# Stationary weights for the grouped queries and the indexer, 512-column scores, and weight conversions ranked 1,000 instructions ahead, in a four-layer hybrid decoder on one core

## The chip, the core and the metric

The kernel runs on one core of a Trainium2 chip. The metric is device time in microseconds (us). TensorE (PE in the rows, PEld for its weight loads) does the matrix products, VectorE (DVE) and ScalarE (ACT) the elementwise work, GpSimd (POOL) and SyncE (SP) issue most of the DMAs.

## The reference

Four layers run on a sequence of 256 tokens of width 2048, with mixers in the order latent attention, sparse attention, sliding window, latent attention. All is float32.

```python
for i in range(DEPTH):                      # 4 layers
    h = rmsnorm(x, norm_in[i])
    # kind 0: latent attention; kind 1: sparse (indexer + top-k); kind 2: window of 128
    self_out, mq, gate = mixer(h @ w_in)    # 32 heads of 64 (kinds 1, 2) or 16 of 128 (kind 0)
    mem_out = memory_attention(mq, mem_n @ w_mem_kv[i])   # 4 heads of 256
    y = concatenate([self_out, mem_out]) * silu(gate)
    x = x + y @ w_out[i]
out = rmsnorm(x, final_norm)

# indexer of kind 1: 16 heads of 64, one shared key
dots  = einsum('bqhd,bkd->bqhk', iq, ik) * 64 ** -0.5
score = einsum('bqhk,bqh->bqk', relu(dots), iw) * 16 ** -0.5
# a query sees its best 64 keys under the causal mask
```

## The kernel before

**Split products.** Each float32 operand is split in a high part of type float32r (11 mantissa bits) and the rest, and a product of two operands is three float32r products: high by high, high by low, low by high. For weights, `parts_of` (L234) does it: ACT copies a 128x512 piece of the landed tile `wr` to `wh` (L60, called by `split`), and DVE writes `wl = wr - wh` (L69). `wh` and `wl` have three buffers each; a piece is converted into a buffer when the products that read the piece three before it are done.

**Two ways to project.** `rows_by` (L240) holds the activations stationary and moves 512 columns of weights: six products of 512 columns for each 128 rows of weights. Its result has tokens on the partitions, and what attention needs with features on the partitions goes through transposes. `columns_by` (L270) holds 128 columns of weights stationary and moves the 256 tokens: for `wh` the high and low part of the tokens in one product of 512 columns (L285), for `wl` the high part alone, 256 columns (L289). Its result has features on the partitions.

**Order.** A layer is six parts: memory heads (part 4), four groups of self heads (0 to 3), memory heads (part 5). A part is a projection with its gate (`project`, `gate`), an attention (`attend`), and one part later its share of the output projection (`w_out`, L1141), which reads the part's gated output `y`: four steps of 128 rows of `w_out`, of which the first two need the first half of `y`, the last two the second half. The program is not run in the order written: a scheduler orders each engine's instructions by a priority that follows the written order and by what is ready in its own model. So the attention of one part lies between the projection and output products of its neighbours. Each engine then runs its list strictly in that order.

**Attention.** `masked_softmax` (L515) works on two blocks of 128 queries, `b` = 0 and 1: score on PE, add of the bias and minimum on DVE (L529), exponential on ACT, reciprocal on DVE, scaling on ACT, then three transposes on PE (L502, tile `ptp`), a split of the transposed weights (tiles `pT`, `pT2`), and the products with the values (tile `o`). For block 0 the score moves both key parts in one product of 256 columns and DVE adds the two halves (L527); for block 1 it is two products of 256 columns into the same columns. `memory_attend` (L576) does six products of 256 columns for each block.

**Grouped layers** (`Grouped`, kinds 1 and 2). `project` (L925) uses `rows_by` for the 512 query columns of a group (tile `acc_q`), ACT scales the rows, and `four_heads` (L461) transposes them in float32 and splits. The indexer (`select`, L817) projects its 1024 query columns with `rows_by` in three calls of 512, 256 and 336 columns (tile `acc_iq`; the last carries the keys and the head weights); for the first two calls the first 64 tokens, which need no selection, are left out. `stacked`, `stacked_late` and `dup` split and transpose.

Of the kernel before, what the change touches and what calls it, by code (L numbers as in the profile page):

```python
# [31 lines left out]
def kernel(ctx: ExitStack, tc: tile.TileContext, a: dict, out: bass.AP,  # L32
# [20 lines left out]
    def f32(ap):  # L53
        return ap.bitcast(F32)
# [185 lines left out]
    def rows_by(xt, kts, w, k0, cols, name, prepare=None, each=None, late=None):  # L240
# [3 lines left out]
        for s in range(0, kts, ST):  # L244
# [3 lines left out]
            for k in range(m):  # L248
# [4 lines left out]
                for t in range(2):  # L253
                    xh, xl = (q[:, v, (s + k) % 4, t * P:(t + 1) * P] for v in range(2))
                    first, last = s + k == 0, s + k == kts - 1
                    if late is not None and t == 0:

                        both = late[:, s + k].rearrange("p v c -> p (v c)")
                        if not last:
                            nc.tensor.matmul(acc[t][:, :n], both, wh[:, :n], start=first, stop=False)  # L260
                        nc.tensor.matmul(acc[t][:64, :n], both[:, :64], wl[:, :n], start=False, stop=False)
                        if last:
                            nc.tensor.matmul(acc[t][:, :n], both, wh[:, :n], start=False, stop=True)
                        continue
# [43 lines left out]
    class Norm:  # L308
# [37 lines left out]
        def finish(self):  # L346
# [5 lines left out]
            nc.vector.tensor_scalar(self.eighth, self.rstd, 0.125, None, op0=OP.mult)  # L352
            half = small("xh", 2)
# [161 lines left out]
    def masked_softmax(score, bias, scale=None, nsk=None):  # L515
# [5 lines left out]
        for b in range(2):  # L521
# [54 lines left out]
    def memory_attend(nm, kT, v, qT, gT):  # L576
        y = act.tile([P, 2, 4, S], F32R, name="y", tag="y", bufs=2)
        for h in range(2):
            es = []
            mn, sm = small("mn", 2), small("sm", 2)  # L580
            for b in range(2):
                sp = misc("msp")
                qs = slice(b * P, (b + 1) * P)
                seq = [(qT[h][:, u, k, qs], kT[h][:, v_, k, :])
                       for k in range(2) for u, v_ in ((0, 0), (0, 1), (1, 0))]
                for n_, (l, r_) in enumerate(seq):
                    nc.tensor.matmul(sp[:, :S], l, r_, start=n_ == 0, stop=n_ == len(seq) - 1)
                nc.vector.tensor_reduce(mn[:, b:b + 1], sp[:, :S], AX.X, OP.max, negate=True)
# [3 lines left out]
                nc.scalar.activation(e, sp[:, :S], AF.Exp, bias=ms[:, :1], scale=nm.col("rstd", b),  # L592
# [640 lines left out]
```

## Time and profile before

| | |
|---|---|
| device time, median of 3 runs | 2577.18 us (2577.11 to 2577.99) |
| span of the profiled execution | 2575.1 us |
| PE busy | 2564.1 us |
| PEld busy | 2208.4 us |
| DVE busy | 1906.1 us |
| ACT busy | 1621.0 us |
| DMA | 520.02 MB, mean 202 GB/s |

The span runs from the first to the last instruction of one profiled execution; no other time of that execution is given, and the median of the runs is 2.1 us more than the span, for what lies around it. PE is busy in all but 11 us of it. A busy PE is one with products in flight; how fast they follow each other is read from their starts.

### The profile page before, as it was taken

The numbers are of one execution on the slowest core, as the hardware profiler recorded it, in microseconds if no ns is written. First come the engines' busy times: TensorE is split into PE (matmuls) and PEld (weight loads), VectorE is DVE, ScalarE is ACT, GpSimd is POOL, SyncE is SP. The second block draws the span as 40 slices with busy tenths as digits, with TensorE's granted clock in tenths as the row PEclk, the third lists the DMA queues.
The fourth block names the chain that finished last, engine by engine and source line by source line (L and its number), as shares of the span: only waits on it lengthen the run. The fifth ranks groups of instructions, "written<-read, shape, count | busy, mean of one in ns | idle before, by whom it ended". The sixth has DMA issues, their size and how long they took to land. (4 is left out here: it accounts for less than half of the span.)

```text
span 2575.1 us, 41628 instructions
## 1 busy us (share of the span) xinstructions
PE 2564.1 (100%) x13986; PEld 2208.4 (86%) x13986; DVE 1906.1 (74%) x4179; ACT 1621.0 (63%) x3467; POOL 87.1 (3%) x159
## 2 busy tenths in 40 slices
PE   9999999999999999999999999999999999999998
PEld 7888898888888888888888888888889888888887
DVE  6666667677777786887778776787878767777776
ACT  6556556556656566667666666676766655665665
POOL 1000000000000000000000000000000000000000
PEclk9999999999999999999999999999999999999999
DMA  9888777666676667566656575555655877676664
GB/s 303 258 259 267 239 212 235 185 170 191 196 201 201 203 213 246 173 197 188 196 165 197 170 226 170 169 183 185 196 156 148 241 201 198 196 196 181 212 173 179
DMA packets 459416, 520.02 MB, mean 202 GB/s; under 512 B 69520, under 2 KB 353056, under 8 KB 457536
## 3 DMA queue, kind: packets, MB, share of 16 engines
q1 hardware_dynamic: 441744, 449.72, 58.3%
q0 software_dynamic: 16736, 66.65, 8.0%
q8 instruction: 110, 1.80, 0.3%
q14 instruction: 106, 0.87, 0.1%
q10 hardware_dynamic: 720, 0.98, 0.1%
HBM read 494.10 MB, written 35.75 MB: 206 GB/s over the span
## 5 line engine op out<-in xcount | busy, mean ns | idle before, releaser
L69 DVE TENSOR_TENSOR wl<-wr,wh 128x512 fp32r<-128x512 f32 (+2 forms) x1720 | 1159.4, 677 | 579.1 <-ACT wh L60 555.5
L60 ACT ACTIVATE wh<-wr 128x512 fp32r<-128x512 f32 (+2 forms) x1720 | 1064.9, 621 | 801.7 <-PE acc_g L285 166.9
L285 PE MATMUL acc_g<-xT,wh 128*128 128x512 f32 x1536 | 484.7, 396 | 0.0
L289 PEld LDWEIGHTS acc_g<-xT,wl 128*128 128x128 f32 x1536 | 284.6, 188 | 63.0
L289 PE MATMUL acc_g<-xT,wl 128*128 128x256 f32 x1536 | 304.6, 280 | 0.0
L266 PE MATMUL acc_wo<-wl,y 128*128 128x512 f32 x752 | 297.3, 395 | 0.3 <-DVE wl L69 0.3
L267 PE MATMUL acc_wo<-wh,y 128*128 128x512 f32 x752 | 292.4, 390 | 0.0
L285 PEld LDWEIGHTS acc_g<-xT,wh 128*128 128x128 f32 x1536 | 235.9, 189 | 1.3
L265 PE MATMUL acc_wo<-wh,y 128*128 128x512 f32 x752 | 234.9, 392 | 0.1
L266 PEld LDWEIGHTS acc_wo<-wl,y 128*128 128x128 f32 x752 | 141.3, 188 | 28.5 <-DVE wl L69 1.2
L267 PEld LDWEIGHTS acc_wo<-wh,y 128*128 128x128 f32 x752 | 141.4, 188 | 27.1
L265 PEld LDWEIGHTS acc_wo<-wh,y 128*128 128x128 f32 x752 | 139.3, 188 | 28.5 <-ACT y L60 1.0
L285 PE MATMUL acc_mk<-mT,wh 128*128 128x512 f32 x512 | 161.5, 396 | 0.4 <-ACT wh L60 0.4
L285 PE MATMUL acc_mq<-xT,wh 128*128 128x512 f32 x512 | 161.6, 396 | 0.0
L1146 DVE TENSOR_TENSOR x<-x,acc_wo 128x512 f32<-128x512 f32 x184 | 122.3, 682 | 4.0 <-PE acc_wo L267 3.6
L285 PE MATMUL acc_qn<-cT,wh 128*128 128x512 f32 x384 | 121.3, 397 | 0.0
L285 PE MATMUL acc_cq<-xT,wh 128*128 128x512 f32 x384 | 120.9, 396 | 0.0
L289 PEld LDWEIGHTS acc_mk<-mT,wl 128*128 128x128 f32 x512 | 96.1, 188 | 22.8 <-DVE wl L69 0.4
L289 PEld LDWEIGHTS acc_mq<-xT,wl 128*128 128x128 f32 x512 | 93.7, 188 | 19.6
L289 PE MATMUL acc_mq<-xT,wl 128*128 128x256 f32 x512 | 103.4, 282 | 0.0
L266 PE MATMUL acc_q<-wl,xT 128*128 128x512 f32 x256 | 101.4, 396 | 0.0
L289 PE MATMUL acc_mk<-mT,wl 128*128 128x256 f32 x512 | 101.1, 278 | 0.0
(335 smaller groups left out, 4349.5 us busy)
## 6 DMA issues: line engine op xcount, KB each, us to landing
wr<-in_w_out_dram SPq DMA_DIRECT2D x188, 512.0 KB, 3.7
wr<-in_w_in_a_dram SPq DMA_DIRECT2D x176, 512.0 KB, 4.0
wr<-in_w_mem_kv_dram SPq DMA_DIRECT2D x120, 512.0 KB, 4.5
wr<-in_w_in_b_dram SPq DMA_DIRECT2D x112, 512.0 KB, 3.5
wr<-in_w_in_c_dram SPq DMA_DIRECT2D x104, 512.0 KB, 3.5
wr<-in_w_uq_dram SPq DMA_DIRECT2D x192, 128.0 KB, 2.9
wr<-in_w_uq_dram SPq DMA_DIRECT2D x48, 256.0 KB, 3.8
tab<-flat POOLq DMA_DIRECT2D x8, 1536.0 KB, 9.1
```

The costliest lines, as they stand in the source:

```text
L60: inst = nc.scalar.activation(o, i, AF.Copy, scale=scale)
L69: nc.vector.tensor_sub(lo, src, f32(hi))
L265: nc.tensor.matmul(acc[t][:, :n], xh, wh[:, :n], start=first, stop=False)
L266: nc.tensor.matmul(acc[t][:, :n], xh, wl[:, :n], start=False, stop=False)
L267: nc.tensor.matmul(acc[t][:, :n], xl, wh[:, :n], start=False, stop=last)
L285: nc.tensor.matmul(acc[j], wh[:, o:o + P], q[:, :, kt % 4, :], start=kt == 0, stop=False)
L289: nc.tensor.matmul(acc[j][:, 0, :], wl[:, o:o + P], q[:, 0, kt % 4, :], start=False, stop=kt == kts - 1)
L1146: nc.vector.tensor_add(xs, xs, acc[t])
```

## The change

`Grouped.project` calls `columns_by` twice for the 512 query columns and a new `heads_by_columns`, which adds the two halves of the result, scales and splits them; the float32 transposes of the queries go. The indexer calls a new `columns_of`, which is `columns_by` with a list of column tiles and a first token for each: 384 and 192 moving columns for the query tiles (tokens 64 to 255), 512 and 256 for the tile with keys and head weights. Scores of block 1 move both key parts in one product of 512 columns, and DVE adds the halves (in `memory_attend` after a copy on ACT). The instructions of `parts_of` get a rank 1,000 instructions earlier than their place in the program.

```diff
 def parts_of(wr, c0, n):
     ...
-        split(wh[:, :n], wl[:, :n], wr[:, c0:c0 + n])
+        with tc.high_priority(offset=1000):
+            split(wh[:, :n], wl[:, :n], wr[:, c0:c0 + n])
...
+    def columns_of(xt, kts, w, c0, tiles, name):
+
+        acc = [ps.tile([P, 512], F32, name=f"acc_{name}{j}", tag="acc", bufs=4) for j in range(len(tiles))]
+        n = tiles[-1][0] + tiles[-1][1]
+        per, each = ST * 512 // n, 512 // n
+        for s in range(0, kts, per):
+            m = min(per, kts - s)
+            wr, _ = stage(w, s, m, (c0, n))
+            other_work()
+            for k2 in range(0, m, each):
+                wh, wl = parts_of(wr, k2 * n, each * n)
+                for k in range(each):
+                    kt = s + k2 + k
+                    q = xt[kt // 4]
+                    for (o, width, r0), at in zip(tiles, acc):
+                        nc.tensor.matmul(at[:width, :2 * (S - r0)], wh[:, k * n + o:k * n + o + width],
+                                         q[:, :, kt % 4, r0:], start=kt == 0, stop=False)
+                    for (o, width, r0), at in zip(tiles, acc):
+                        nc.tensor.matmul(at[:width, :S - r0], wl[:, k * n + o:k * n + o + width],
+                                         q[:, 0, kt % 4, r0:], start=False, stop=kt == kts - 1)
+        return acc
...
 masked_softmax
-            if b == 0:
-                nc.vector.tensor_add(u[:, :n], sp[:, n:2 * n], bi)
-                bi = u[:, :n]
-            nc.vector.tensor_tensor_reduce(u[:, :n], sp[:, :n], bi, -1.0,
+            nc.vector.tensor_add(u[:, :n], sp[:, n:2 * n], bi)
+            nc.vector.tensor_tensor_reduce(u[:, :n], sp[:, :n], u[:, :n], -1.0,
...
 memory_attend
-                seq = [(qT[h][:, u, k, qs], kT[h][:, v_, k, :])
-                       for k in range(2) for u, v_ in ((0, 0), (0, 1), (1, 0))]
...
+                for k in range(2):
+                    nc.tensor.matmul(sp, qT[h][:, 0, k, qs], kT[h][:, :, k, :], start=k == 0, stop=False)
+                    nc.tensor.matmul(sp[:, :S], qT[h][:, 1, k, qs], kT[h][:, 0, k, :], start=False, stop=k == 1)
+                u = wk.tile([P, S], F32, name="u", tag="e", bufs=4)
+                copy_act(u, sp[:, S:])
+                nc.vector.tensor_tensor_reduce(u, sp[:, :S], u, -1.0, BIG,
...
 Latent.attend, block 1
-                        seq = [(q[:, 0, z, qs], k[:, 0, z, :]), (q[:, 0, z, qs], k[:, 1, z, :]),
-                               (q[:, 1, z, qs], k[:, 0, z, :]),
-                               (qr[:, h, qs], self.kr[:, 0, :]), (qr[:, h, qs], self.kr[:, 1, :])]
+                        seq = [(q[:, 0, z, qs], k[:, :, z, :]), (q[:, 1, z, qs], k[:, 0, z, :]),
+                               (qr[:, h, qs], self.kr)]
...
 Grouped.select (stacked, stacked_late and late_x go)
+            for h0 in range(0, 16, 4):
+                tiles = [(0, P, 64), (P, P, 64)] + ([(S, 80, 0)] if h0 == 12 else [])
+                acc = columns_of(nm.at, 16, w, 2560 + h0 * 64, tiles, "iq")
...
+        def heads_by_columns(self, dst, acc):
+
+            zs = part_tile(F32)[:].rearrange("p (j c) -> p j c", j=2)
+            for j in range(2):
+                copy_act(zs[:, j, :], acc[j][:, 1, :])
+                nc.vector.tensor_add(zs[:, j, :], zs[:, j, :], acc[j][:, 0, :])
+            eighth = self.nm.half[:, None, :].to_broadcast([P, 2, S])
+            nc.vector.scalar_tensor_tensor(zs, zs, 0.25, eighth, op0=OP.mult, op1=OP.mult)
+            for h, main, low in ((0, slice(0, 64), slice(64, P)), (1, slice(64, P), slice(0, 64))):
+                copy_act(dst[main, h::2, :], zs[main])
+                nc.vector.tensor_sub(dst[low, h::2, :], zs[main], f32(dst)[main, h::2, :])
+
         def project(self, g):
             nm = self.nm
-            acc = rows_by(nm.at, 16, self.w, 0, (g * 512, 512), "q")
...
             for z in range(2):
-                rows_ = part_tile(F32)
-                for t in range(2):
-                    copy_act(rows_[:, t * S:(t + 1) * S], acc[t][:, z * S:(z + 1) * S],
-                             scale=nm.col("eighth", t))
-                four_heads(q[z], [rows_[:, t * S:(t + 1) * S] for t in range(2)])
+                acc = columns_by(nm.at, 16, self.w, 0, (g * 512 + z * S, S), "q")
+                self.heads_by_columns(q[z], acc)
...
 Grouped.attend
-                    if b == 0:
-                        nc.tensor.matmul(sp[:, :S], qb, self.k[:, g, :, :P], start=True, stop=True)
-                    else:
-                        for v in range(2):
-                            nc.tensor.matmul(sp[:, :S], qb, self.k[:, g, v, :],
-                                             start=v == 0, stop=v == 1)
+                    n = (b + 1) * P
+                    nc.tensor.matmul(sp[:, :2 * n], qb, self.k[:, g, :, :n], start=True, stop=True)
```

The built programs show how the scheduler's order moves. The first place is PE in the sparse layer, where one part's output projection begins (`acc_wo`; `y_13987` before and `y_13980` after are that part's output, `o_14191` and `o_14184` the values' products of its last heads). Before:

```order
L979 MATMUL o_14191<-pT2_14227,vz_12691 128x512
L979 MATMUL o_14191<-pT2_14226,vz_12692 128x512
L979 MATMUL o_14191<-pT2_14226,vz_12691 128x256
L979 MATMUL o_14191<-pT2_14227,vz_12691 128x256
L979 MATMUL o_14191<-pT2_14226,vz_12692 128x256
L950 MATMUL sp_14919<-kd_11111,qS_14643 128x256
L285 MATMUL acc_g0_14794<-xT_10871,wh_14888 128x512
L285 MATMUL acc_g1_14795<-xT_10871,wh_14888 128x512
L953 MATMUL sp_14928<-kd_11111,qS_14643 128x256 x2
L265 MATMUL acc_wo0_15199<-wh_15203,y_13987 128x512
```

After the change, at the same transition, in the second step of the output projection and behind it:

```order
L259 MATMUL acc_wo1_15223<-wh_15236,y_13980 128x512
L257 MATMUL acc_wo0_15270<-wh_15274,y_13980 128x512
L258 MATMUL acc_wo0_15270<-wl_15275,y_13980 128x512
L259 MATMUL acc_wo0_15270<-wh_15274,y_13980 128x512
L518 MATMUL ptp_14247<-ident_81,e_14232 128x128
L951 MATMUL sp_14942<-kd_11099,qS_14458 128x256
L951 MATMUL sp_14951<-kd_11099,qS_14458 128x512
L518 MATMUL ptp_14247<-ident_81,e_14241 128x128 x2
L257 MATMUL acc_wo1_15271<-wh_15274,y_13980 128x512
L258 MATMUL acc_wo1_15271<-wl_15275,y_13980 128x512
L259 MATMUL acc_wo1_15271<-wh_15274,y_13980 128x512
L976 MATMUL o_14184<-pT2_14219,vz_12654 128x512
```

Before, the last heads' value products stand ahead of the part's first output product; after, two steps of the output projection and the start of another column (`acc_wo0_15270`) stand ahead of them, and steps three and four of the first column follow later.

The second place is ACT at the same transition. Before:

```order
L60 ACTIVATE wh_14888<-wr_14874 128x512
L60 ACTIVATE wh_15203<-wr_15201 128x512
L60 ACTIVATE wh_15213<-wr_15201 128x512
L60 ACTIVATE y_13987<-yt_14266 128x512
L60 ACTIVATE wh_15225<-wr_15223 128x512
L60 ACTIVATE z_14900<-acc_g0_14794 128x256
L60 ACTIVATE wh_15235<-wr_15223 128x512
```

After:

```order
L60 ACTIVATE wh_15236<-wr_15224 128x512
L60 ACTIVATE wh_15248<-wr_15246 128x512
L60 ACTIVATE z_14923<-acc_g0_14817 128x256
L60 ACTIVATE pT2_14219<-ptp_14215 128x3x128
L60 ACTIVATE wh_15258<-wr_15246 128x512
L548 ACTIVATE e_14232,sm_14224<-u_14227,mn_14223 128x128
L60 ACTIVATE wh_15274<-wr_15272 128x512
L548 ACTIVATE e_14241,sm_14224<-u_14236,mn_14223 128x256
```

Here `wh_15248` and `wh_15258` are steps three and four of the first column. They are converted ahead of the exponentials of the last heads (`e_14232`, `e_14241`), from which the second half of `y` comes, and `wh_15274` then takes the buffer of `wh_15236`.

## Rows read from the trace of the kernel before

**Rows 1.** The page: engine totals, granted clock in 40 slices.
```profile
PE 2564.1 (100%) x13986; PEld 2208.4 (86%) x13986; DVE 1906.1 (74%) x4179; ACT 1621.0 (63%) x3467; POOL 87.1 (3%) x159
...
PEclk9999999999999999999999999999999999999999
```

**Rows 2.** All waits of PE: what waited for what, us in total, times, longest.
```profile
PE wu L102 <- DVE ones L98: 1.1, 1, 1.1
PE acc_mv L265 <- ACT wh L60: 0.6, 1, 0.6
PE acc_mk L285 <- ACT wh L60: 0.4, 1, 0.4
PE acc_wo L266 <- DVE wl L69: 0.3, 2, 0.2
```

**Rows 3.** Two windows, 96 row products (acc_mv) and 128 column products (acc_mk).
```profile
98.46:120.25 21.79, 21.79 (x98) 18.03 (x97) 13.69 (x24) 12.65 (x24) 0.53 (x1) 1.00 0.78 264
120.25:142.53 22.28, 22.28 (x129) 19.45 (x128) 15.12 (x27) 13.73 (x28) 1.59 (x3) 1.00 0.85 262
```

**Rows 4.** Timeline of PE: float32 transposes between products (start us, us, what).
```profile
1226.75 0.49 PE L502 MATMUL ptp<-ident,e 128*128 128x128 f32 x3
...
1227.32 0.39 PE L267 MATMUL acc_wo<-wh,y 128*128 128x512 f32 x1
```

**Rows 5.** Counts: query products and float32 transposes of the grouped layers.
```profile
L266 PE MATMUL acc_q<-wl,xT 128*128 128x512 f32 x256 | 101.4, 396 | 0.0
...
L467 PE MATMUL tr<-ident,hl 128*128 128x128 f32 x64 | 8.9, 272 | 0.0
```

**Rows 6.** Timeline of PE in the indexer, 336 columns; then of PEld, two loads.
```profile
1018.05 0.32 PE L267 MATMUL acc_iq<-wh,xT 128*128 128x336 f32 x1
...
1019.89 0.32 PE L267 MATMUL acc_iq<-wh,xT 128*128 128x336 f32 x1
...
1017.48 0.19 PEld L266 LDWEIGHTS acc_iq<-wl,xT 128*128 128x128 f32 x1
1017.59 0.19 PEld L267 LDWEIGHTS acc_iq<-wh,xT 128*128 128x128 f32 x1
```

**Rows 7.** Timeline of PE, ACT and DVE where the sparse layer ends.
```profile
1440.24 0.39 PE L267 MATMUL acc_wo<-wh,y 128*128 128x512 f32 x1
1440.46 1.23 PE L979 MATMUL o<-pT,vz 128*128 128x512 f32 x6
1441.53 0.64 PE L265 MATMUL acc_wo<-wh,y 128*128 128x512 f32 x2
1442.32 0.51 PE L266 MATMUL acc_wo<-wl,y 128*128 128x512 f32 x1 [0.15 <-DVE wl L69]
1442.66 0.39 PE L267 MATMUL acc_wo<-wh,y 128*128 128x512 f32 x1
...
1443.12 0.40 PE L267 MATMUL acc_wo<-wh,y 128*128 128x512 f32 x1
1443.58 0.50 PE L265 MATMUL acc_wo<-wh,y 128*128 128x512 f32 x1
...
1440.71 0.64 ACT L60 ACTIVATE wh<-wr 128x512 fp32r<-128x512 f32 x1 [0.20 <-ACT th L483]
...
1441.58 0.68 DVE L69 TENSOR_TENSOR wl<-wr,wh 128x512 fp32r<-128x512 f32 x1
```

**Rows 8.** Timeline of PE and ACT: one head from score to scaled weights, little queued.
```profile
1187.16 0.40 PE L953 MATMUL sp<-kd,qS 128*128 128x256 f32 x2
1187.40 0.40 PE L289 MATMUL acc_g<-xT,wl 128*128 128x256 f32 x2
...
1190.19 0.80 ACT L60 ACTIVATE e<-e,rc 128x128 f32<-128x128 f32 x2 [0.23 <-DVE rc L552]
```

**Rows 9.** Groups of DVE: the add of a bias and a score, 256 columns.
```profile
L962 DVE TENSOR_TENSOR bs<-bm,vs 128x256 f32<-128x256 f32 x32 | 13.4, 417 | 0.0
```

**Rows 10.** Window over two parts of the sparse layer.
```profile
1136.00:1300.00 164.00, 164.00 (x850) 139.07 (x850) 131.45 (x319) 112.80 (x259) 3.94 (x6) 1.00 0.63 198
```

More of the change, by code (lines that the diff above doesn't have):

```diff
@@ L255, in rows_by @@
                     first, last = s + k == 0, s + k == kts - 1
[L256 to L264, printed above, removed]
                     nc.tensor.matmul(acc[t][:, :n], xh, wh[:, :n], start=first, stop=False)
@@ L352, in finish @@
             nc.vector.tensor_scalar(self.eighth, self.rstd, 0.125, None, op0=OP.mult)
+            self.neg = small("xn", 2, bufs=3)
+            nc.vector.tensor_scalar(self.neg, self.rstd, -1.0, None, op0=OP.mult)
             half = small("xh", 2)
@@ L583, in memory_attend @@
                 qs = slice(b * P, (b + 1) * P)
-                seq = [(qT[h][:, u, k, qs], kT[h][:, v_, k, :])
-                       for k in range(2) for u, v_ in ((0, 0), (0, 1), (1, 0))]
-                for n_, (l, r_) in enumerate(seq):
-                    nc.tensor.matmul(sp[:, :S], l, r_, start=n_ == 0, stop=n_ == len(seq) - 1)
-                nc.vector.tensor_reduce(mn[:, b:b + 1], sp[:, :S], AX.X, OP.max, negate=True)
+                for k in range(2):
[4 more added lines that the diff above has]
+                nc.vector.tensor_tensor_reduce(u, sp[:, :S], u, -1.0, BIG,
+                                               op0=OP.add, op1=OP.min, accum_out=mn[:, b:b + 1])
                 ms = small("ms", 2)
@@ L737, in score @@
                     else:
[L738 to L740 removed]
+                        seq = [(q[:, 0, z, qs], k[:, :, z, :]), (q[:, 1, z, qs], k[:, 0, z, :]),
+                               (qr[:, h, qs], self.kr)]
                     for n_, (l, r_) in enumerate(seq):
[L742 removed]
+                        n = r_.shape[-1] * (r_.shape[1] if len(r_.shape) == 3 else 1)
+                        nc.tensor.matmul(sp[:, :n], l, r_, start=n_ == 0, stop=n_ == 2)
                     return sp
@@ L852, in select, with indexer_keys @@
             return self.selection(iqT, ikd, iw, iw2)
-        def stacked_late(self, dst, src, sc, n):
-            s64 = small("s64", 1)
-            nc.scalar.activation(s64[:64], sc[64:], AF.Copy)
-            lo = tmp("lo")
-            nc.scalar.activation(lo[:64, :n * 64], src[64:], AF.Copy)
-            z = tmp("zq")
-            nc.vector.tensor_add(z[:64, :n * 64], lo[:64, :n * 64], src[:64])
-            s3 = z[:64, :n * 64].rearrange("p (g d) -> p g d", g=n)
-            for g0 in range(0, n, 4):
-                hl = part_tile()[:64].rearrange("p (g v d) -> p g v d", g=4, v=2)
-                copy_act(hl[:, :, 0, :], s3[:, g0:g0 + 4], scale=s64[:64])
-                nc.vector.scalar_tensor_tensor(hl[:, :, 1, :], s3[:, g0:g0 + 4], s64[:64], f32(hl)[:, :, 0, :],
-                                               op0=OP.mult, op1=OP.subtract)
-                tp = misc("tr", F32R)
-                for g in range(4):
-                    nc.tensor.transpose(tp[:, g * 64:g * 64 + 64], hl[:, g].rearrange("p a b -> p (a b)"),
-                                        identr[:64, :64])
-                copy_act(dst(g0, g0 + 4), f32(tp)[:, :S].rearrange("p (j c) -> p j c", c=64))
+        def indexer_keys(self, ikd, iw, acc):
+            nm = self.nm
+            z = wk.tile([P, S], F32, name="z", tag="z", bufs=3)
+            copy_act(z[:80], acc[:80, S:])
+            nc.vector.tensor_add(z[:80], z[:80], acc[:80, :S])
+            tp = misc("tp")
+            for t in range(2):
+                nc.tensor.transpose(tp[:, t * P:t * P + 80], z[:80, t * P:(t + 1) * P], ident[:80, :80])
+            for t in range(2):
+                copy_act(iw[:, t * 16:(t + 1) * 16], tp[:, t * P + 64:t * P + 80], scale=nm.col("rstd", t))
+                nc.vector.tensor_scalar(iw[:, t * 16:(t + 1) * 16], iw[:, t * 16:(t + 1) * 16],
+                                        nm.col("rstd", t), 0.25, op0=OP.mult, op1=OP.mult)
+            zs = wk.tile([P, S], F32, name="zs", tag="z", bufs=3)
+            nc.vector.scalar_tensor_tensor(zs[:64], z[:64], 2.0, nm.half[:64], op0=OP.mult, op1=OP.mult)
+            for rows in (slice(0, 64), slice(64, P)):
+                copy_act(ikd[rows, 0, :], zs[:64])
+                nc.vector.tensor_sub(ikd[rows, 1, :], zs[:64], f32(ikd)[:64, 0, :])
         def selection(self, iqT, ikd, iw, iw2):
```

47 lines of the change are left out of this document (12 added, 35 removed).

## The prediction

> **What bounds the kernel now.** I read the page first: PE is busy 2564.1 of 2575.1 us, at the full granted clock in every slice [rows 1]. Busy only means that products are in flight, so I read PE's waits next: they come to 2.4 us in all, most of them in the first 30 us [rows 2]. So the time is the sum of the spacings at which products follow each other, and two things can change it: the number and form of PE's instructions, and stops that PE doesn't have now. DVE (74%) and ACT (63%) have room on the mean [rows 1]. The sum starts at the runs' median, 2577.2; the profiled span is 2.1 us below it, and I take that difference as fixed.
>
> **Spacings.** In a window of row products alone, 96 of them take 21.79 us, .227 each. The next window has 128 column products, half with 512 and half with 256 columns: 22.28 us, .348 a pair [rows 3], so about .230 and .118. Twelve products of 336 columns go from 1018.05 to 1019.89, .153 each [rows 6]. Three float32 transposes and one product of .23 take 1226.75 to 1227.32, so a transpose takes .11 [rows 4].
>
> **Queries.** Each of eight group projections (two layers, four groups) goes from 96 row products to 128 column products: 22.28 for 21.79, together +3.9. The 64 float32 transposes go [rows 5]: 64 x .11 = -7.0. Sum -3.1, with -2 to -4 as bounds, since the windows are from another stage.
>
> **Indexer.** Before: 80 products of 512 columns (18.2), 80 of 256 (9.4), 96 of 336 (14.7), and 36 small transposes without a row of their own, between nothing and .11 each; I take 2.5, as they move float32r. That is 44.8 us. After: 128 of 384 columns, on the line from 336 to 512 at .173; 128 of 192; 16 pairs at .348; two transposes. For 192 the trace has no product. Below, the line goes on to .092; above is the 256 at .118. Two weight loads that follow each other directly start .11 apart (1017.48 and 1017.59) [rows 6], and each product here has its own load, so I take .11: 22.1 + 14.1 + 5.8 = 42.0, which is -2.8. The ends are -1.8 (.118) and -5.1 (.092).
>
> The Trainium skill, "TensorE: Matmul & The Clock Gate", section "LDWEIGHTS (loading the stationary operand)", says that a load takes its columns over 1.2 GHz: 107 ns for 128, whatever is streamed. That speaks against cutting the moving side to 192 columns, and the two loads .11 apart agree. By it the 192-column products take .107 and the indexer saves 3.2 instead of 2.8; by the streaming line alone it would be 5.1.
>
> **Scores.** 64 grouped blocks go from two products of .118 to one of .230; 32 memory blocks from six of .118 to two pairs of .348; 32 latent blocks from five of .118 to .230 + .118 + .230. Each of the three saves .4, together -1.2 (0 to -2).
>
> PE's work thus falls by 7.1 (4 to 11).
>
> **What DVE and ACT get.** A grouped head gets one more DVE add of .417 [rows 9], a memory block an ACT copy, a query half two more adds and a scaling. Nothing waits for these directly while attention runs far behind PE; two parts of the sparse layer have DVE at 131.45 of 164 us [rows 10]. The DMAs carry the same bytes in other pieces, and PE's waits name no DMA [rows 2]: nothing.
>
> **The ranking.** It can remove little: PE waits for a conversion only at the start, which stays, and at two layer ends. There PE stops for `wl`: the two products that read `wh` start at 1441.53, the next should come .46 later and comes at 1442.32, and its successor .34 instead of .23 later; then 1443.12 to 1443.58 loses as much again [rows 7]. That is .78 at one place, 1.6 for both.
>
> What it adds is seen in the order. A conversion no longer ranks by when its product is wanted. Before, the last heads' value products stand ahead of their part's output projection, whose four steps then run through. After, conversions push ahead of the exponentials on ACT; the output projection starts while the last pair of heads is unfinished, steps three and four are converted though the half of `y` that they need isn't there, and these two tiles hold two of three buffers. PE goes on with another column on the third buffer alone: `wh_15274` takes that of `wh_15236`, and their products stand next to each other. Conversion is then in the open.
>
> How long it takes is in the trace [rows 7]. The last product on the old tile makes way at 1440.46, ACT has the new `wh` at 1441.35, DVE the `wl` at 1442.26, the product on it starts at 1442.32: .89 for `wh`, 1.86 for `wl`. Before, 1.07 us of other products stood between. I went through the order after the change and counted, for each tile, the PE work between the buffer's last reader and the new tile's first:
>
> - four places with none (three transitions of the sparse or the window layer as shown, one more in the window layer). The `wl` is wanted .23 after the `wh`: 1.86 - .23 = 1.63. Conversion alone would be .2 less when DVE is free; 1.6 each, 6.4.
> - three places with .67: once 1.86 - .67 - .23, twice 1.86 - .67 - .46; with the .11 after a stop 1.1 + .8 + .8 = 2.7.
> - sixteen with .8 to 1.04 (before: two, at .78 each). Most follow a stop just ahead, in which the conversion proceeds; I take .2 each, 3.2.
> - One softmax: at the first transition of the sparse layer only .9 us of PE work stands between a head's scores and its transposes. The least queued head in the trace takes from 1187.40 to 1190.6 for the first block's scaled weights and 1190.99 for both [rows 8], 3.2 and 3.6. Less .9, less the 1.1 already counted there, and with the added DVE add of .4: 1.6. Before, no head has under 5.7 us of work in this place.
>
> New stops: 13.9. Lower bound: the four at .9 for the bare ACT conversion and little else, 4. Upper: the four at 2.5 with a queue on DVE, the three at 1, the sixteen at .78, the softmax at 3, 28.
>
> **Sum.** 2577.2 - 7.1 - 1.6 + 13.9 = 2582.4. **I forecast 2582 us, slightly slower.** Measured runs lie within .9 us of each other, and I count a difference of 0.2% (5.2 us) as the least that can be told from no change.
>
> **Rivals.**
>
> *The stops are hidden, the work saved counts.* If the real engines run further ahead than I count, or DVE and ACT take the tight stretches faster, only the lower bound of the stops is left: 2577.2 - 7.1 - 1.6 + 4 = 2572.5, and 2568.5 with none. For it speaks that nearly all distances in the order are as before (median 3 us) and that before lost under 2 us this way. Against it that the two places in before with one us of work between did lose time, and these have none. It decides if a stop at a bare buffer costs under .9. 18%.
>
> *DVE becomes the bound of the grouped layers.* Per part 8 adds of .417 and two query halves at some 1.7 are 6.7 us; two parts go from 131.45 to about 145 of 164 us, 88%. At that share chains of short instructions queue, and the waits spread beyond the places counted. If a quarter of the 53 us that eight parts add were exposed, 13 us more: 2595. Against it: DVE is still short of full. 9%.
>
> *Products under 256 columns run slower.* The trace has no float32r product below 256 columns other than transposes. At the rate of a float32 transpose (.11 for 128 columns) 192 columns take .165, 7 us more: 2589. At twice that .33, 28 more: 2610. 9%.
>
> *That the change doesn't do what it says* is excluded by the order for its form: the transposes are gone, the scores merged.
>
> **How the numbers follow.** The forecast (stops outweigh or match the work saved, 2573 to 2592) has 64%, of which 34 within 0.2% (2572 to 2582.3) and 30 above. The first rival is faster, 18%; the other two are slower, 18% together. So faster .18, same .34, slower .48. The range 2570 to 2595 leaves out half of the third rival, the tail of the second and the bottom of the first, about 2 in 10. The forecast's own range is 2573 to 2592.
>
> **What would show it.** Right: PE waits on `wh` and `wl` of `acc_wo` of 8 to 15 us, in the sparse and window layers, at the part transitions; a pure query window of 22.3 us for 128 products; 192-column products .105 to .12 apart; the layer-end stops smaller. Wrong: no PE waits over 4 us in all, which gives the first rival; waits spread over the scores and transposes of all heads, the second; 192-column products above .16, the third. A lower granted clock after the stops, which I don't expect from stops of 1 to 3 us, would make all of it wrong.

## The result, and the profile after

The changed kernel takes 2606.05 us (median of 4 runs, 2603.82 to 2608.85) against 2577.35: 1.0111 times as long, interval 1.0099 to 1.0122. The forecast was 2582 with a range up to 2595, so it is slower by 28.7 us where 5 were forecast. The profiled execution has a span of 2602.0 us, 26.9 more than before.

The page of the changed kernel, engine totals:

```profile
PE 2571.8 (99%) x13984; PEld 2201.8 (85%) x13984; DVE 1958.3 (75%) x4366; ACT 1629.7 (63%) x3492; POOL 82.5 (3%) x151
```

PE is busy 7.7 us longer [rows 1] though it has less to do, and the span has grown by 26.9: PE now stands. All of its larger waits (what waited for what, us in total, times, longest):

```profile
PE acc_wo L257 <- ACT y L60: 6.9, 6, 1.7
PE acc_wo L257 <- ACT wh L60: 3.9, 4, 1.2
PE ptp L518 <- ACT e L60: 3.0, 3, 2.5
PE acc_wo L258 <- DVE wl L69: 2.6, 8, 0.5
PE ptp L518 <- ACT u L60: 1.1, 2, 0.9
PE wu L102 <- DVE ones L98: 1.1, 1, 1.1
```

With the small ones they come to 22.0 us, where before had 2.4 [rows 2]. The largest is one that the prediction does not have: products of the output projection that wait for `y`, the gated output of their own part.

Idle time is not all that a stop costs, since the products ahead of it drain and those behind it come slowly at first. So I took every spacing from one product's start to the next, less the median for the same two forms (over the profiles of five runs, stretches of low clock left out), and summed in three groups:

```
                              before    after    difference
medians (the work)            2540.1   2531.1     -9.0
late behind an idle time         2.7     29.6    +26.9   (idle alone 1.5 -> 21.4)
late at the lower clock          0.0      5.3     +5.3
all other deviations            22.5     27.0     +4.5
first to last product         2565.3   2593.0    +27.7
```

The work fell, a little more than forecast. The stops cost 27 us where the forecast had 12.3 net, and the clock, which the forecast left alone, costs 5.3. By what ended them, the 29.6 us are: 11.3 for `wh` and `wl` in the grouped layers, 8.0 for `y`, 4.8 for the softmax, and 5.5 for others, most of them at the start of the program and in other layers.

One stop of each kind shows how. The one that the prediction counted, PE's timeline at the second transition of the sparse layer (start, duration, what, in brackets the idle time before it and what ended it):

```profile
1288.17 0.39 PE L259 MATMUL acc_wo<-wh,y 128*128 128x512 f32 x1
1289.32 0.50 PE L257 MATMUL acc_wo<-wh,y 128*128 128x512 f32 x1 [0.77 <-ACT wh L60]
1290.05 0.50 PE L258 MATMUL acc_wo<-wl,y 128*128 128x512 f32 x1 [0.23 <-DVE wl L69]
```

Starts that should lie .23 apart lie 1.15 and .73 apart: 1.4 us late.

Then the first transition of the sparse layer, around 1208 us: PE, and then DVE and ACT.

```profile
1206.08 0.50 PE L258 MATMUL acc_wo<-wl,y 128*128 128x512 f32 x1 [0.33 <-DVE wl L69]
1206.42 0.40 PE L259 MATMUL acc_wo<-wh,y 128*128 128x512 f32 x1
1209.28 0.47 PE L518 MATMUL ptp<-ident,e 128*128 128x128 f32 x1 [2.46 <-ACT e L60]
...
1211.04 0.63 PE L258 MATMUL acc_wo<-wl,y 128*128 128x512 f32 x1
1211.47 0.63 PE L259 MATMUL acc_wo<-wh,y 128*128 128x512 f32 x1
```

```profile
1205.34 0.69 DVE L69 TENSOR_TENSOR wl<-wr,wh 128x512 fp32r<-128x512 f32 x1
1205.94 0.42 DVE L959 TENSOR_TENSOR bs<-bm,vs 128x256 f32<-128x256 f32 x1
1206.28 0.55 DVE L69 TENSOR_TENSOR pT<-ptp,pT 128x384 fp32r<-128x384 f32 x1
1206.74 0.41 DVE L542 TENSOR_TENSOR u<-sp,bs 128x256 f32<-128x256 f32 x1
1207.19 0.42 DVE L543 CUSTOM_DVE_ANT_0 u<-sp,u 128x256 f32<-128x256 f32 x1
...
1207.72 0.51 ACT L548 ACTIVATE e<-u,mn 128x256 f32<-128x256 f32 x1 [1.61 <-DVE mn L543]
...
1208.84 0.79 ACT L60 ACTIVATE e<-e,rc 128x128 f32<-128x128 f32 x2
```

DVE works without a break from 1205.34 to 1207.6. A head's scores have been there since 1205.0, and the second of them stands behind a conversion, its bias and another head's split. The added add (L542, 256 columns, .41 us) is one of the five. ACT stands 1.61 us for it, then PE 2.46.

The granted clock in windows of 2 us there (busy time of PE, clock, DMA share, GB/s):

```profile
1206.00:1208.00 2.00, 0.73 (x2) 0.96 0.74 253
1208.00:1210.00 2.00, 0.72 (x3) 0.50 0.77 227
1210.00:1212.00 2.00, 2.00 (x7) 0.50 0.80 289
1212.00:1214.00 2.00, 2.00 (x8) 0.50 0.02 8
1214.00:1216.00 2.00, 1.90 (x7) 0.83 0.12 7
```

During the stop the clock falls to the lower of its two levels, 1.2 GHz, and stays there for some 5 us after PE is busy again; products of 512 columns then start .43 apart (1211.04, 1211.47) in place of .23. The same happens at two transitions of the window layer; windows of 6 us there (PE, PEld, DVE, ACT, POOL, clock, DMA share, GB/s):

```profile
1711.00:1717.00 6.00, 4.90 (x16) 3.80 (x16) 3.49 (x13) 3.19 (x10) 0.00 (x0) 0.72 0.00 0
1865.00:1871.00 6.00, 5.13 (x16) 3.00 (x16) 3.79 (x14) 2.84 (x8) 0.00 (x0) 0.72 0.94 335
```

Then the wait for `y`, at the second transition, in the timeline of all engines:

```profile
1294.23 0.63 PE L257 MATMUL acc_wo<-wh,y 128*128 128x512 f32 x2
...
1295.39 0.40 PE L259 MATMUL acc_wo<-wh,y 128*128 128x512 f32 x1
1295.86 0.29 DVE L959 TENSOR_TENSOR bs<-bm,vs 128x128 f32<-128x128 f32 x1 [1.32 <-DMA bm<-tab]
1296.07 0.68 DVE L982 TENSOR_TENSOR yt<-o,gT 128x512 f32<-128x512 f32 x1
...
1296.79 0.63 ACT L60 ACTIVATE y<-yt 128x512 fp32r<-128x512 f32 x1 [2.97 <-DVE yt L982]
...
1297.47 0.50 PE L257 MATMUL acc_wo<-wh,y 128*128 128x512 f32 x1 [1.68 <-ACT y L60]
```

DVE's list has the first bias of the next part (L959) ahead of the gated product `yt` (L982) of this one. That bias waits 1.32 us for the DMA of the bias table `bm`. It has one buffer and is loaded when the last head of the part before has read it. `yt` stands behind the wait, `y` behind `yt`, PE behind `y`. There are five such waits of DVE for the table, 6.5 us; before has none.

### The profile page after: what moved, and what is told of

It is laid out like the page before. It is cut to its first block, busy times and chain, and to the rows that moved or that the text cites. A ratio compares the mean times of both kernels' runs of the same rounds, so it can differ in the third digit from the quotient of the medians.

```text
span 2602.0 us, 41888 instructions
## 1 busy us (share of the span) xinstructions
PE 2571.8 (99%) x13984; PEld 2201.8 (85%) x13984; DVE 1958.3 (75%) x4366; ACT 1629.7 (63%) x3492; POOL 82.5 (3%) x151
## 4 chain that ended last, share of the span: by engine, by line
PE 85%; issue 12%; DMA 2%; DVE 1%; ACT 0%; POOL 0%; POOLq 0%; ACTq 0%; DVEq 0%; SPq 0%
PE acc_g L277 11%; PE acc_g L281 6%; PE acc_wo L257 5%; PE acc_wo L258 5%; PE acc_wo L259 5%; PE acc_mk L277 5%; PE acc_mq L277 5%; PE acc_cq L277 3%; PE acc_qn L277 3%; PE acc_mq L281 2%; PE acc_q L277 2%; PE acc_mk L281 2%; PE acc_mv L258 2%; PE acc_mv L257 2%; PE acc_mv L259 2%
## 5 line engine op out<-in xcount | busy, mean ns | idle before, releaser
L60 ACT ACTIVATE wh<-wr 128x512 fp32r<-128x512 f32 (+1 forms) x1712 | 1064.1, 623 | 812.7 <-PE acc_g L277 173.9
L69 DVE TENSOR_TENSOR wl<-wr,wh 128x512 fp32r<-128x512 f32 (+1 forms) x1712 | 1158.9, 680 | 546.1 <-ACT wh L60 518.6
L259 PE MATMUL acc_wo<-wh,y 128*128 128x512 f32 x752 | 291.6, 391 | 0.0
L257 PE MATMUL acc_wo<-wh,y 128*128 128x512 f32 x752 | 243.5, 400 | 11.6 <-ACT y L60 6.9
L257 PEld LDWEIGHTS acc_wo<-wh,y 128*128 128x128 f32 x752 | 137.7, 190 | 44.2 <-ACT y L60 11.3
L277 PE MATMUL acc_q<-xT,wh 128*128 128x512 f32 x512 | 161.1, 396 | 0.0
L281 PEld LDWEIGHTS acc_q<-xT,wl 128*128 128x128 f32 x512 | 94.4, 188 | 21.9 <-DVE wl L69 1.2
```

The source lines that it names most:

```text
L60: inst = nc.scalar.activation(o, i, AF.Copy, scale=scale)
L69: nc.vector.tensor_sub(lo, src, f32(hi))
L257: nc.tensor.matmul(acc[t][:, :n], xh, wh[:, :n], start=first, stop=False)
L259: nc.tensor.matmul(acc[t][:, :n], xl, wh[:, :n], start=False, stop=last)
L277: nc.tensor.matmul(acc[j], wh[:, o:o + P], q[:, :, kt % 4, :], start=kt == 0, stop=False)
```

## The experiments

The theory of the prediction: the conversions that are ranked ahead make the stops. The rival, formed when the order without the ranking showed the same places without work, is this: the queries and the scores each give DVE more to do in every part of a grouped layer; the attention of a part then ends later, behind the start of its own output projection, and the stops follow from that. One number of the built order shows it. It is the PE work (by the spacings of the prediction) from a part's last value product to its first output product, for eight parts in the two grouped layers; negative, where the output projection begins first:

```
run                          median (least, most)   PE waits   time, median
before                        -0.2  (-3.7,  1.9)       2.4      2577.3
only_indexer                  -0.2  (-3.7,  1.9)       2.9      2573.6
wide_scores_no_add            -0.2  (-3.7,  1.9)       2.1      2576.7
latent_scores_alone           -0.2  (-3.7,  1.9)       3.5      2576.7
only_memory_scores            -0.2  (-3.7,  1.9)       5.0      2580.5
rank_alone                    -0.9  (-4.6,  1.9)       2.4      2578.6
longer_chain_on_act           -2.8  (-6.8,  1.9)       4.2      2581.7
only_queries                  -4.4  (-5.7,  1.7)       7.1      2582.0
indexer_and_queries           -4.4  (-5.7,  1.7)       7.3      2578.0
no_rank                       -5.7  (-7.8,  0.1)      23.3      2602.8
only_mixer_scores             -6.3  (-6.8, -5.4)      15.3      2601.0
the change                    -6.4  (-7.8,  0.1)      22.0      2606.1
bias_table_early              -6.4  (-7.8,  0.1)      19.2      2599.3
idle_dve_work                 -6.8  (-8.6, -6.7)      24.2      2613.3
indexer_relieved_queries       5.3  (-2.3,  6.9)       3.3      2592.0
indexer_relieved_gates         7.0  ( 2.8,  7.4)       3.9      2588.8
```

**The change without its ranking.**
```diff
-        with tc.high_priority(offset=1000):
-            split(wh[:, :n], wl[:, :n], wr[:, c0:c0 + n])
+        split(wh[:, :n], wl[:, :n], wr[:, c0:c0 + n])
```


> The changed kernel without the ranking of the conversions; all else as changed. If the ranking makes the stops, as the prediction has it: PE waits fall from 21.8 to about 3 us and the time is about 2570. If the longer attention work on DVE makes them (the queries and the scores each add DVE work to every grouped head, and the end of a part's attention slides into its output projection), the waits stay near 20 us and the time near 2604; the order of this kernel has the same four places with no PE work between a buffer's last and next reader.

2602.8 us, 1.0101 (1.0086 to 1.0116), PE waits 23.3 us. The stops are all there without the ranking, so the ranking theory falls.

**One part alone on the kernel before: queries, mixers' scores, indexer.** Each is the part of the change's diff that its name says.

> The kernel before with only the stationary-weight queries of the grouped layers. Ranking theory: 3.1 us of PE work less and no new stops, 2574. DVE theory: stops at the part transitions of the grouped layers; the order has one place with no work and three more under .5 us, so some 6 to 10 us of stops, 2580 to 2584.

2582.0 us, 1.0018 (1.0009 to 1.0027). The work falls: the 64 transposes take 6.3 us out, the products put 2.8 in, -3.4 where -3.1 was forecast. The stops give back 6.2, and small deviations the other 2.

> The kernel before with only the 512-column scores of the grouped and latent mixers (64 grouped and 32 latent blocks; memory scores stay). Ranking theory: .8 us less, 2576.4, no new stops. DVE theory: each grouped head has one more DVE add of .417, and stops come at the same transitions; the order has nine places under .5 us, so some 10 to 18 us, 2586 to 2594.

2601.0 us, 1.0092 (1.0077 to 1.0107), more than either theory had: .8 us of PE's work costs 24. Its two largest waits of PE:

```profile
PE acc_wo L265 <- ACT y L60: 5.0, 4, 1.2
PE acc_wo L265 <- ACT wh L60: 4.2, 7, 1.0
```

> The kernel before with only the stationary-weight indexer. Both theories: no new stops, 2.8 us of PE work less, 2574.4; products of 192 columns .105 to .12 apart. If it takes more than 2577, narrow products cost more than the prediction has.

2573.6 us, .9986 (.9977 to .9996): faster than both kernels, and the best of all that were run. Timeline of PE there:

```profile
1003.07 0.54 PE L299 MATMUL acc_iq<-xT,wh 128*128 128x384 f32 x2
1003.44 0.36 PE L302 MATMUL acc_iq<-xT,wl 128*128 128x192 f32 x2
1003.64 0.54 PE L299 MATMUL acc_iq<-xT,wh 128*128 128x384 f32 x2
```

A set of two products of 384 and two of 192 takes .57; the forecast's .173 and .110 give .566.

**Only the DVE add, and only the form.** The first leaves the add away and keeps the wide product; the low part of the keys is then missing from the scores of the second 128 queries. The second keeps the kernel before and adds one DVE instruction per head that nobody needs. The third lengthens a head's chain on ACT.

```diff
 wide_scores_no_add, on only_mixer_scores
-            nc.vector.tensor_add(u[:, :n], sp[:, n:2 * n], bi)
+            if b == 0:
+                nc.vector.tensor_add(u[:, :n], sp[:, n:2 * n], bi)
+                bi = u[:, :n]
 idle_dve_work, on the kernel before
+            else:
+                bx = tmp("bx")[:, :n]
+                nc.vector.tensor_tensor(bx, bi, bi, op=OP.max)
+                bi = bx
 longer_chain_on_act, on the kernel before
+            if b == 1:
+                copy_act(u[:, :n], sp[:, :n])
+                s_ = u
```


> The 512-column scores of the grouped and latent mixers again, but the added DVE add for the second 128 queries is left out, so the low part of the keys is missing from those scores. If the DVE add makes the stops: none, PE waits of 2 to 3 us, 2576 to 2577, for the scheduler's order is then that of the kernel before. If the form of the product makes them (a wider product, a PSUM bank read in another way): near 2601.

2576.7 us, .9998 (.9989 to 1.0007): no stops. The form of the product costs nothing.

> The kernel before with one useless DVE instruction per head (the maximum of the bias with itself, 256 columns, ready long before the score, so that no step of a head waits for it); PE's work is that of before. If DVE's load is what delays a part's attention: stops as with the 512-column scores, 2593 to 2606, with up to 12 places of under .5 us of PE work between two uses of a buffer. If the length of a head's chain does it: no change, 2577.

2613.3 us, 1.0139 (1.0123 to 1.0154), more than expected: 96 added DVE instructions of .42 us, which touch no product of PE, raise DVE's busy time by 31 us and cost 36. The expectation has them ready long before the score. In the trace that holds in the window layer for 25 of 32 heads, where the added instruction ended 6.5 to 45 us before the head's score; that layer, from the last output product of the sparse layer to the first `acc_cq` of the latent layer behind it, took 15.7 us longer (523.7 for 508.0), with 9.7 us of waits on PE where before had .2. For those heads it is DVE's load and not a longer chain. In the sparse layer the instruction stands behind the head's own bias and ended after the score in all 32 heads, so that there it lengthened the chain as well. Its waits on PE are of the change's kinds:

```profile
PE acc_wo L265 <- ACT wh L60: 8.3, 12, 1.0
PE acc_wo L265 <- ACT y L60: 7.5, 6, 1.9
PE acc_wo L266 <- DVE wl L69: 3.2, 5, 1.9
```

> The kernel before with one more step on each head's chain, but on ACT: the score of the second 128 queries is copied from PSUM before DVE reads it. If DVE's load is the cause: the window layer keeps its order, the sparse layer has three tight places, 2577 to 2584. If the length of the chain is the cause: as with the 512-column scores, near 2600.

2581.7 us, 1.0017 (1.0008 to 1.0027). A longer chain costs 4.4 us, where the scores, which lengthen it on DVE, cost 23.8 and the useless DVE instructions 36. So most of it is DVE's load.

> The kernel before with only the conversions ranked 1,000 instructions ahead. By the prediction's theory 2577 plus some 10 us of stops; by the DVE theory no change within 1.5 us, 2576 to 2578.5, since the order's distances between two uses of a buffer stay as they were.

2578.6 us, 1.0005 (.9996 to 1.0014): no difference that can be told. The two stops at the layer ends, which the ranking was to remove, are still there (`acc_wo` waits for `wl` twice, .3 us, as in before).

**DVE relieved.** Two kernels take the gates, and the first the queries too, as three products of 256 columns into the same PSUM columns, so that no halves are left to add. The other two show what they are compared with.

```diff
+                        if narrow:
+                            for v in range(2):
+                                nc.tensor.matmul(acc[j][:, 0, :], wh[:, o:o + P], q[:, v, kt % 4, :],
+                                                 start=kt == v == 0, stop=False)
+                            continue
 gate
-                z = total(acc[j])
-                nc.vector.tensor_mul(hz, z, nm.half)
+                nc.vector.tensor_mul(hz, acc[j][:, 0, :], nm.half)
```


> The kernel before with the indexer and the queries with stationary weights, but gates and queries as three products of 256 columns into the same PSUM columns, so that DVE has no halves to add (nor ACT to copy). PE's time for these is as before if three of .116 stand for one of .233 and one of .117; DVE loses four adds of .417 for each gate. DVE theory: no stops at the transitions but one (the order has one place with no work, about 1.6 us), so 2577.3 - 2.8 - 3.5 + 2 = 2573, between 2570 and 2575. If 256-column products with a load each follow each other slower than .116 (1,536 more of them), the time is longer by 1.5 us for each .001.

2592.0 us, 1.0057 (1.0045 to 1.0070).

> As the run beside it but with the queries as in the kernel before: indexer with stationary weights and gates as three products of 256 columns. DVE theory: no stops, not at the two layer ends either (their 1.6 us go): 2577.3 - 2.8 - 1.6 = 2573, at 2571 to 2574; under the indexer's 2573.6 by 0 to 2.

2588.8 us, 1.0045 (1.0031 to 1.0058).

Both are slower than expected, and by the mechanism that the first expectation names, though at three times its price: 1.5 us for each .001 would be 6 us at .120. A window with 192 gate products there, and one with the 128 products that do the same in only_indexer (PE, PEld, DVE, ACT, POOL, clock, DMA share, GB/s):

```profile
1545.39:1568.42 23.03, 23.03 (x194) 23.03 (x193) 13.64 (x24) 11.35 (x21) 0.00 (x0) 1.00 0.62 185
```
```profile
1535.54:1557.83 22.29, 22.29 (x130) 19.45 (x129) 14.23 (x26) 11.93 (x23) 0.00 (x0) 1.00 0.64 189
```

Three products of .120 take .360, where the pair takes .348; over the 1,536 tiles of the gates that is some 18 us. But the stops went as the DVE theory has it: waits on PE of 3.3 us with the queries in, where the same kernel with DVE's adds has 7.3, and one of .8 at the transitions, where its order has the one place without work:

```profile
PE acc_wo L256 <- ACT wh L60: 0.8, 1, 0.8
```

> Indexer and queries as in the change, gates as before. DVE theory: the sum of the two alone, 2573.6 + 4.7 = 2578.3, with stops at the transitions as with the queries alone.

2578.0 us, 1.0002 (.9993 to 1.0011), the sum of the two alone.

> The kernel before with only the memory scores in 512 columns. The order has eight places of .8 to 1.04 us where before had two: PE work .4 us less, stops some 1 to 3 us more, 2577 to 2580.

2580.5 us, 1.0012 (1.0003 to 1.0021): slower, with PE waits of 5.0. The transitions are as before; more than half of its waits is at the start of the program, which is not explained.

**Which layers, and relief by GpSimd.**

```diff
 latent_scores_alone, on the kernel before, and the latent scores of the change
-            if b == 0:
+            if b == 0 or scale is not None:
 gates on GpSimd
-                nc.vector.tensor_mul(hz, z, nm.half)
+                nc.gpsimd.tensor_mul(hz, z, nm.half)
-                nc.vector.scalar_tensor_tensor(gT[:, 2 * h + j, :], th, 1.0, hz, op0=OP.add, op1=OP.mult)
+                nc.gpsimd.tensor_mul(th, th, hz)
+                nc.gpsimd.tensor_add(gT[:, 2 * h + j, :], th, hz)
```


> The kernel before with the 512-column scores, and their DVE add, in the two latent layers alone (32 blocks). If DVE has room there: no new stops and .4 us less PE work, 2576.5 to 2577.5, and the 24 us of the mixers' scores come from the two grouped layers alone. If any added DVE work costs: a third of the added adds are here, so about 2585.

2576.7 us, .9998 (.9989 to 1.0007). DVE has room in the latent layers; the 24 us come from the grouped ones.

> The 512-column scores of the mixers, which took 2601.0, with the gates' last steps (one product with the scale before the tanh, one product and one add behind it) on GpSimd in place of two DVE instructions for each of 96 tiles. PE's work is the same. If DVE's load makes the stops they shrink: the order has three places under .5 us in place of nine, so 2583 to 2592. If not: 2601.

2604.5 us, 1.0105 (1.0091 to 1.0119): a miss.

> Indexer and queries as in the change, which took 2578.0, with the gates' last steps on GpSimd. If DVE's load makes the stops: one place without work is left of five under .9, some eleven of .9 to 1.04 us; 2572 to 2576. If not: 2578.

2579.4 us, 1.0007 (.9998 to 1.0016): a miss.

> The indexer alone, which took 2573.6, with the gates' last steps on GpSimd. It has only two small stops to lose, at the layer ends, and one place with no work in its order: 2572.5 to 2575.5.

2581.2 us, 1.0016 (1.0007 to 1.0025): a miss, 7.6 us over the indexer alone.

The relief was none. In the first of the three the order hardly moved back: by the same count as in the table, but with spacings from the traces, the distance is -6.1 (-6.6 to -5.4) with the gates on GpSimd, as without, and PE's waits come to 18.6 us. In the third the order is near that of before (.9, from -3.6 to .9), and PE waits 7.1 us all the same, where the indexer alone has 2.9. What DVE gained is seen in its rows. Groups of DVE's conversions by line, without and with the gates on GpSimd (only_mixer_scores, scores_gates_on_gpsimd):

```profile
L69 DVE TENSOR_TENSOR wl<-wr,wh 128x512 fp32r<-128x512 f32 x1624 | 1115.9, 690 | 545.2 <-ACT wh L60 525.1 <-PE acc_g L285 3.3 <-PE acc_mq L285 3.1
```
```profile
L69 DVE TENSOR_TENSOR wl<-wr,wh 128x512 fp32r<-128x512 f32 x1624 | 1156.5, 715 | 558.7 <-ACT wh L60 533.6 <-PE acc_g L285 5.8 <-PE acc_mq L285 4.2
```

Of the 80.7 us that left DVE, 40.6 came back in these conversions alone, and its busy time fell by 8.9 us only. One of them beside GpSimd, in the timelines of DVE and GpSimd:

```profile
1141.41 1.24 DVE L69 TENSOR_TENSOR wl<-wr,wh 128x512 fp32r<-128x512 f32 x1
```
```profile
1141.30 0.79 POOL L485 TENSOR_TENSOR gT<-th,hz 128x256 f32<-128x256 f32 x1
1142.06 1.19 POOL L484 TENSOR_TENSOR th<-th,hz 128x256 f32<-128x256 f32 x1
```

The Trainium skill, "GPSIMD Engine Reference", section "1. Specifications", says that GpSimd shares its SBUF interfaces with VectorE and contends with DVE instructions that have two SBUF inputs. `wl = wr - wh` is one, and the trace agrees: the row shown takes 1.24 us, the 185 conversions of this run that lie beside such GpSimd work take .91 on the mean, the other 1,439 take .69.

**The table in time.** The bias table in two halves with a buffer and a DMA each, so that heads 0 to 3 of the next part can be loaded while heads 4 to 7 still read theirs. The places of PE's products at the transitions are those of the kernel that it is made from.

```diff
-            bm = act.tile([P, 8, S], F32, name="bm", tag="big3")
+            bm = [act.tile([P, 8, S], F32, name="bm", tag="big3")[:, :4],
+                  act.tile([P, 4, S], F32, name="bm", tag="aux", bufs=AUX)]
```


> The changed kernel with the bias table of a part in two tiles, heads 0 to 3 and 4 to 7, each with its own DMA and its own buffer, so that the first half can be loaded while the last four heads of the part before still read theirs. PE's order stays as it was at the transitions. In the profile of the changed kernel DVE waits 6.5 us for this table at five transitions, and the gated product of the part before, from which y comes, stands behind that wait. If the table is a cause: DVE's waits on bm vanish, PE's waits for y fall from 6.9 us to about 2, and the time falls by 5 to 8 us, to 2598 to 2601. If the stops come from DVE's load alone: PE waits for something else as long, and the time stays at 2604 to 2606.

2599.3 us, 1.0084 (1.0070 to 1.0098), 6.7 under the change by the medians; the runs of each spread over 4 to 5 us, and the two profiled executions are 3.7 apart. DVE has no wait for the table left. PE's largest:

```profile
PE acc_wo L257 <- ACT wh L60: 3.9, 4, 1.2
PE acc_wo L257 <- ACT y L60: 3.7, 5, 1.7
PE ptp L518 <- ACT e L60: 3.0, 3, 2.5
```

The wait for `y` fell from 6.9 to 3.7, not to 2. So the table is a cause of about half of that wait; the waits for `wh` and `e` are untouched by it.

> Indexer and queries (2578.0) with the bias table in two halves likewise. DVE waits 1.0 us for the table there, once: 2576.5 to 2578 if the table is a cause, 2578 if not.

2577.1 us, .9998 (.9989 to 1.0007), as if the table's single wait there were worth its 1.0; within what can be told.

## Why the prediction was wrong

**The step that failed** is the first of "What it adds": "A conversion no longer ranks by when its product is wanted" as the reason why the output projection begins while the last heads are unfinished. The order that it read was right, the edit that it blamed was not. Ranking alone adds 1.3 us, too little to tell from nothing, and the change without it takes 2602.8. With it fails the sentence under "What DVE and ACT get" by which the sum has no term for the added DVE work: "Nothing waits for these directly while attention runs far behind PE". The DVE add of the mixers' scores alone costs 24 us: 2601.0 with it, 2576.7 without. Five edits stood in that order at once, and two of them, the queries and the scores, load DVE in every part of the grouped layers. Before, a part's last value product lay within 4 us of its first output product in all eight parts: there was no room for later attention. The prediction took the last value products to stand ahead of the output projection; in the trace of before that holds in four of the eight parts, and in the other four the projection begins 1.1 to 3.7 us of work earlier. The parts of the change alone add up: queries +4.7, mixers' scores +23.8, memory scores +3.2, indexer -3.7, ranking +1.3 make 29.3, against 28.7 for all together.

**What was right.** PE's work: -7.1 forecast, -9.0 measured, the queries within .3 us and the indexer within 1.0 (its small transposes take 3.0 and not 2.5). Narrow products: .104 on the mean at 192 columns, which ends the third rival. The price of a stop at a bare buffer: 1.6 forecast where nothing stands between, 1.4 and .1 behind it measured at the place shown. The conversions' share as a whole: 13.9 less the 1.6 of a softmax is 12.3, against 11.3. That is in part luck, since the ranking did not make them; and by the prediction's own sign, waits of `acc_wo` on `wh` and `wl` of 8 to 15 us, they are 6.5 (3.9 and 2.6).

**What was left out.** The waits for `y` (8.0 late) and most of those for the softmax (4.8, against 1.6): the sum asked of each buffer when it comes free, and did not ask of `y` when its last head is done, though the order showed the output projection ahead of that head. A wait for `y` stood in the trace of before already: the second loss at the layer end, 1443.12 to 1443.58, which the prediction books as one for a conversion, has this row in the timeline of PEld:

```profile
1443.58 0.19 PEld L265 LDWEIGHTS acc_wo<-wh,y 128*128 128x128 f32 x1 [0.50 <-ACT y L60]
```

So part of the 1.6 us that the ranking was to remove was no conversion, and ranking alone removed nothing of the rest. Behind the late `y` of the change stood a transfer that the sum priced at nothing, since no engine waited for it before: the bias table, late as soon as the heads that free its buffer are late. "The DMAs carry the same bytes in other pieces ... nothing" looked at bytes and not at the buffer's release.

**The clock.** The prediction said that a lower clock after the stops would make all of it wrong, and did not expect it. It came three times, 5.3 us.

**The rivals.** "DVE becomes the bound of the grouped layers" (2595, 9%) names the cause, with a price of a quarter of 53 us. In the place it was wrong: the waits don't spread over all heads, they gather at the transitions, where late attention meets the projection that needs it. A share of busy time said little: DVE's was 80% in two parts before [rows 10] and in the same window after it is 134.00 of 164, 82%, since the stops stretch the parts; with the useless DVE instructions it is 126.38, less than before.

**Still open.** In every run with more than 8 us of waits the order had already moved, because the scheduler counts DVE's load too. Whether the chip with the old order and the added DVE work would have stopped was not tried, since the order follows from the program. The indexer with its gates on GpSimd comes nearest: an order near the old one, DVE's conversions slowed, and 4.2 us more of waits; how much of its 7.6 us comes from the slower steps of the gate itself (three of .89 to .96 us on GpSimd for two of .42 on DVE) is not shown. The rest of PE's wait for `y`, the 4.5 us of small deviations, and the waits of only_memory_scores are not accounted for.

## What to carry to other kernels

A row of PE at 100% tells nothing of how closely the other engines keep up: look for the last instruction that a stage needs and how far ahead of its use it lies, and price work added to any engine by that distance. Where an order moves under several edits, build it for each edit alone before naming the cause. Merging two products of 256 columns into one of 512 saves .006 us, and the DVE add that it asks for costs .417: such a trade can pay only where nobody waits for DVE's end, as in the latent layers here, and even there no gain can be told (2576.7 for 2577.3).

## What the runs showed of the hardware

Products of 256 columns with a weight load each follow each other at .1200 us in a long row (192 in 23.03 us, PEld busy all the time), and at .174 on the mean where every other product has 512 columns. The Trainium skill, "TensorE: Matmul & The Clock Gate", section "LDWEIGHTS (loading the stationary operand)", gives a load as its columns over 1.2 GHz, an estimate of 107 ns for 128; here 192 loads stood .120 apart. Products are in flight all through that row too, so no run here shows which of the two bounds it.

GpSimd work beside DVE's two-input conversions lengthened these from .69 to .91 us on the mean, to 1.24 in the row shown, and was no relief for DVE here.

A stop of 2.46 us brought the clock from 2.4 to 1.2 GHz. So did shorter stops that lie close together (1.19 and .47 us around 1865), while only_mixer_scores, with 15.3 us of waits in all, none above 1.25, kept the full clock to the end of its work.
